# The sums and the gated product of a seven-product FFN move from GpSimd to VectorE, and its activation work is issued at fixed distances

## The chip, the cores and the metric

One core of one Trainium2 chip runs the whole program. The metric is device microseconds of one execution; the number quoted is a median over runs. All times are in microseconds (us) unless marked ns.

## The reference

A residual stream of 512 tokens by 1024 features goes through two blocks; all numbers are fp32. The first block is an HGRN2 mixer, a conv FFN, an NSA mixer and a conv FFN. The second is a SwiGLU FFN, a hybrid mixer and a SwiGLU FFN again. Only the two SwiGLU FFNs of the second block are touched by the change:

```python
def swiglu(x, w_gu, w_down):
    g, u = jnp.split(x @ w_gu, 2, axis=-1)
    return (jax.nn.silu(g) * u) @ w_down
```

Here x is 512 by 1024, w_gu is 1024 by 5632 and w_down is 2816 by 1024. The result, halved, is added to the stream.

## The kernel before

**How a product is made.** An fp32 product is made of three matmuls. Each operand is split into a high part in fp32r and the rest (h and l); the products h·h, h·l and l·h are added in PSUM. ScalarE writes the high part of a weight (line 249), VectorE the rest (line 250), so every weight piece costs one instruction on each. An activation is split in the same way (lines 473 and 476).

**The order.** The program writes its order by hand. Every engine runs its own instructions in the order in which the program issued them. Side work is a set of generators; a small queue (Weave) resumes them by a clock that advances with the matmuls issued, so `yield 1.2` means "go on 1.2 us of matmul work later". That clock only decides the order in which instructions stand on each engine.

**The seven products.** In the two SwiGLU FFNs the first two pairs of column tiles (t = 0 and 2) are ordinary: a block for the gate half g and a block for the up half u, evacuated by line 1146 (silu, ScalarE) and line 1168 (product, VectorE). From t = 4 on, that is for 9 of the 11 pairs of each FFN and 18 in all, a 2x2 block product is made with seven half-size products instead of eight (`fm_fast`, lines 463 to 465). This document calls such a pair of tiles a group, and each of the seven products a step. The steps of a group run in the order A11, A12, S2, S1, S3, S4, A22, each of 24 matmuls with 256 columns. They accumulate in the PSUM banks A, F, A, E, A, E, A. The bank A of one step has to be emptied before the step after next may start in it.

Per group the engines around TensorE do this:

- The weights arrive as four raw tiles of 128x1024 (5 buffers). `w_sum` makes four sums or differences of them, S1 to S4 (lines 210, 212, 215, 219; S1 and S2 in `wsum` tiles, S3 and S4 in place), on GpSimd.
- The seven weight pieces are split (lines 249 and 250) six pieces ahead of their use (HL_BUFS = 6).
- The banks are emptied after their steps: line 1109 (ScalarE, after A11), 1115 (ScalarE, after S2), 1112 (ScalarE, after S1), and 1117, 1120, 1122, 1127 (VectorE, after A12, S3, S4 and A22).
- silu runs on ScalarE right behind the VectorE add (lines 1118 and 1123), a product on GpSimd (line 1124), and the two results are split (473, 476) for the down product.

Ahead of the groups, `fast_inputs` makes sums of the normed input (lines 413 and 432 to 435) and splits them into the tiles T, with T_D as the distance between its parts. The stretch in which it runs, from the norm up to the first group, is called the ramp here. The groups come in rounds of 1, 4 and 4, each round followed by the down product, whose evacuation is line 790.

Of the kernel before, what the change touches and what calls it, by code (L numbers as in the profile page):

```python
# [12 lines left out]
F32 = mybir.dt.float32  # L13
F32R = mybir.dt.float32r
I32 = mybir.dt.int32
AF = mybir.ActivationFunctionType
OP = mybir.AluOpType
# [8 lines left out]
HALVES = ((0, 256), (256, 512))  # L26
FULL = ((0, 512),)
RAW_BUFS, SUM_BUFS, HL_BUFS, W2_BUFS = 5, 2, 6, 11
T_D, FAST_FROM = 1.2, 4
HG_D1, HG_D2, HG_D3, HG_D4, HG_D5 = 0.8, 1.9, 1.1, 0.0, 3.1  # L30
NORM_D1, NORM_D1B, NORM_D2, NORM_STEP, NHALF, W_DELAY, NPE = 1.6, 4.5, 1.2, 0.2, 2, 13.0, 7
W_UNIT = 29
# [86 lines left out]
class Builder:  # L119
# [81 lines left out]
    def w_sum(self, g, name):  # L201


        raw = lambda f: self.w_raw[g["load"] + ("A21", "A22", "A11", "A12").index(f)]
        src = g["src"]
        if name in ("S1", "S2"):
            src[name] = self.t([128, 4, 256], "wsum", SUM_BUFS)
        tt = self.nc.gpsimd.tensor_tensor
        if name == "S1":
            tt(src["S1"], raw("A21"), raw("A22"), op=OP.add)  # L210
        elif name == "S2":
            tt(src["S2"], src["S1"], raw("A11"), op=OP.subtract)
        elif name == "S3":
            src["S3"] = raw("A21")
            tt(src["S3"], raw("A11"), src["S3"], op=OP.subtract)
            self.raw_free()
        else:
            src["S4"] = raw("A12")
            tt(src["S4"], src["S4"], src["S2"], op=OP.subtract)
# [184 lines left out]
    def fast_inputs(self, X, tags, first, second):  # L404


        nc = self.nc
        xh, xl = X
        th, tl = self.big(tags[0], F32R), self.big(tags[1], F32R)
        two = lambda t: t.rearrange("p (i t) -> p i t", t=256)  # L410

        def whole(k, lo, f):
            nc.gpsimd.tensor_tensor(two(f), xh[:, k::4, lo:lo + 256].bitcast(F32), xl[:, k::4, lo:lo + 256].bitcast(F32),
                                    op=OP.add)
            return f

        def run():
            yield from self.wv.wait_in(first)
            yield 1.5
            left = []  # L420
            store = self.t([128, 1024], "hmask")
            for k in range(4):
                left.append(whole(k, 0, store[:, k * 512:k * 512 + 512] if k < 2 else self.w2()))
                yield T_D
            yield from self.wv.wait_in(second)
            yield 0.5
            for k in range(4):
                r, q = whole(k, 256, self.w2()), left[k]
                yield T_D
                a, b = self.w2(), self.w2()  # L430
                tt = nc.vector.tensor_tensor
                tt(a[:, 0:256], r[:, 0:256], q[:, 0:256], op=OP.subtract)
                nc.gpsimd.tensor_tensor(a[:, 256:512], r[:, 256:512], r[:, 0:256], op=OP.subtract)
                tt(b[:, 0:256], r[:, 256:512], a[:, 0:256], op=OP.subtract)
                tt(b[:, 256:512], q[:, 256:512], b[:, 0:256], op=OP.subtract)
                for i, f in enumerate((a, b)):
                    self.split(th[:, i * 4 + k, :], tl[:, i * 4 + k, :], f)
                    yield T_D
        return (th, tl), self.wv.spawn(run())

    def fm_fast(self, X, T, blocks, after):
# [643 lines left out]
    def ffn(self, X, waits, up, down, scale, after, conv=None, tags=None):  # L1085

        nc = self.nc
# [5 lines left out]
        pend = []  # L1093

        def fast_group(a, t):

            c = {}
            f = slice(t - a, t - a + 2)
            two = lambda w: w.rearrange("p (m t) -> p m t", t=256)

            def late(lo, src):
                yield 1.2
                self.split(mh[:, f, lo:lo + 256], ml[:, f, lo:lo + 256], two(src))

            def after(step, banks):
                A, E, F = (banks.get(n) for n in "AEF")
                if step == "A11":
                    c["1"] = self.w2()
                    nc.scalar.activation(c["1"], A, AF.Copy)
                elif step == "S1":  # L1110
                    c["5"] = self.w2()
                    nc.scalar.activation(c["5"], E, AF.Copy)
                elif step == "S2":
                    c["2"] = self.w2()
                    nc.scalar.activation(c["2"], A, AF.Copy)  # L1115
                elif step == "A12":
                    nc.vector.tensor_tensor(c["1"], c["1"], F, op=OP.add)
                    nc.scalar.activation(c["1"], c["1"], AF.Silu)
                elif step == "S3":
                    nc.vector.tensor_tensor(c["5"], c["5"], A, op=OP.add)  # L1120
                elif step == "S4":
                    nc.vector.tensor_tensor(c["2"], c["2"], E, op=OP.add)
                    nc.scalar.activation(c["2"], c["2"], AF.Silu)
                    nc.gpsimd.tensor_tensor(c["2"], c["2"], c["5"], op=OP.mult)
                    pend.append(self.wv.spawn(late(256, c["2"]), 1.2))
                else:
                    nc.vector.tensor_tensor(c["1"], c["1"], A, op=OP.mult)
                    pend.append(self.wv.spawn(late(0, c["1"])))
            self.fm_fast(X, T, ((up, 0, 8, t * 128, 256), (up, 0, 8, DFF + t * 128, 256)), after)

        for r, (a, b) in enumerate(self.ROUNDS):
            mh, ml = self.big("b0", F32R), self.big("b1", F32R)
# [997 lines left out]
```

## Time and profile before

| | |
|---|---|
| median of 3 runs | 2788.18 us (2786.33 to 2792.54) |
| the profiled execution: its own time | 2786.39 us |
| the profiled execution: span of its trace | 2784.6 us |
| TensorE busy | 2703.4 us, 97% of the span |
| VectorE, ScalarE, GpSimd busy | 61%, 41%, 19% |
| groups of the two SwiGLU FFNs | 1526 to 1808 and 2450 to 2730 us, with the down products between them |

The span is the time between the first and the last instruction in the trace; the execution took 1.8 us more. Busy shares are averages over stages that have different limits.

### The profile page before, as it was taken

To read this page: it belongs to the slowest core of one execution; us is meant where nothing else is said; L and a number is where in the kernel's file an instruction comes from. 1 tells how busy PE (TensorE), PEld (TensorE's weight loads), DVE (VectorE), ACT (ScalarE), POOL (GpSimd) and SP (SyncE) were. 2 spreads that over 40 slices of the span, in tenths; PEclk is the share of its full clock that TensorE was granted. 3 is DMA by queue.
4 is the path that set the end of the run, shared out by engine and by line. 5 is a ranking of instruction groups with operands and counts; after the bars stand their busy time and mean duration, and the time that the engine had idled before them with its cause. 6 is when DMAs were issued, how large, how long until landed. Compare 5 with 4: busy or idle time off the path is not lost.

```text
span 2784.6 us, 40263 instructions
## 1 busy us (share of the span) xinstructions
PE 2703.4 (97%) x15857; PEld 2358.7 (85%) x15857; DVE 1703.4 (61%) x2867; ACT 1142.0 (41%) x2114; POOL 533.8 (19%) x518
## 2 busy tenths in 40 slices
PE   7999999999999999999999989999999999998999
PEld 5988898888978889888888888897878987988888
DVE  7876567767545896544448675753455235768584
ACT  3323353323323895333344443442356333344343
POOL 3111110000102781000014333310000000425241
PEclk8999999999999999999999999999999999999999
DMA  7642136555231002333221332347535332222321
GB/s 260 191 143 84 46 99 198 178 185 175 64 106 61 1 2 76 100 105 99 91 91 50 110 103 81 106 68 118 95 86 82 60 91 91 69 91 91 106 92 61
DMA packets 257658, 278.94 MB, mean 100 GB/s; under 512 B 16408, under 2 KB 231853, under 8 KB 257469
## 3 DMA queue, kind: packets, MB, share of 16 engines
q1 hardware_dynamic: 229739, 233.23, 30.0%
q10 hardware_dynamic: 27730, 43.14, 5.0%
q8 instruction: 125, 2.05, 0.3%
q14 instruction: 64, 0.52, 0.1%
HBM read 274.23 MB, written 2.10 MB: 99 GB/s over the span
## 4 chain that ended last, share of the span: by engine, by line
PE 82%; DVE 11%; ACT 3%; issue 3%; POOL 1%; DMA 0%; ACTq 0%; DVEq 0%; SPq 0%; POOLq 0%
PE pg L363 20%; PE pg L364 20%; PE pg L366 20%; DVE wl L250 4%; PE pg L463 2%; PE pg L464 2%; PE pg L465 2%; PE pa L891 2%; DVE b L476 2%; ACT wh L249 1%; PE pg L395 1%; PE pg L393 1%; PE pg L394 1%; PE pa L1487 1%; DVE w L534 1%
## 5 line engine op out<-in xcount | busy, mean ns | idle before, releaser
L250 DVE TENSOR_TENSOR wl<-raw,wh 128x512 fp32r<-128x512 f32 (+2 forms) x806 | 649.2, 833 | 341.7 <-ACT wh L249 340.4
L363 PE MATMUL pg<-b,wh 128*128 128x512 f32 (+1 forms) x1856 | 673.5, 364 | 1.0 <-DVE w L1168 1.0
L364 PE MATMUL pg<-b,wl 128*128 128x512 f32 (+1 forms) x1856 | 668.0, 361 | 0.0
L249 ACT ACTIVATE wh<-raw 128x512 fp32r<-128x512 f32 (+2 forms) x806 | 495.7, 657 | 218.5 <-PE pg L366 142.0
L366 PE MATMUL pg<-b,wh 128*128 128x512 f32 (+1 forms) x1472 | 522.8, 357 | 0.0
L363 PE MATMUL pg<-hTh,wh 128*128 128x512 f32 (+2 forms) x1096 | 412.6, 378 | 9.3 <-DVE w L1168 7.3
L364 PE MATMUL pg<-hTh,wl 128*128 128x512 f32 (+2 forms) x1096 | 406.5, 373 | 0.7 <-DVE wl L250 0.5
L366 PE MATMUL pg<-hTl,wh 128*128 128x512 f32 (+2 forms) x1096 | 397.9, 370 | 0.0
L363 PEld LDWEIGHTS pg<-b,wh 128*128 128x128 f32 x1856 | 348.7, 188 | 56.7 <-DVE w L1168 1.4
L364 PEld LDWEIGHTS pg<-b,wl 128*128 128x128 f32 x1856 | 348.8, 188 | 54.7
L366 PEld LDWEIGHTS pg<-b,wh 128*128 128x128 f32 x1472 | 275.1, 188 | 44.1
L495 POOL TENSOR_TENSOR w<-w,w 128x256 f32<-128x256 f32 (+1 forms) x78 | 78.4, 1010 | 1153.5 <-ACT w L494 1152.9
L363 PEld LDWEIGHTS pg<-hTh,wh 128*128 128x128 f32 (+1 forms) x1096 | 206.3, 188 | 54.4 <-issue 12.7
L366 PEld LDWEIGHTS pg<-hTl,wh 128*128 128x128 f32 (+1 forms) x1096 | 203.3, 188 | 40.9 <-DVE hTl L476 0.4
L364 PEld LDWEIGHTS pg<-hTh,wl 128*128 128x128 f32 (+1 forms) x1096 | 206.4, 188 | 35.9 <-DVE wl L250 1.1
L473 ACT ACTIVATE b<-w 128x512 fp32r<-128x512 f32 (+1 forms) x128 | 77.2, 604 | 294.4 <-DVE w L1168 155.8
L463 PE MATMUL pg<-b,wh 128*128 128x256 f32 x576 | 167.5, 291 | 30.8 <-ACT w L1115 23.4
L465 PE MATMUL pg<-b,wl 128*128 128x256 f32 x576 | 165.6, 287 | 0.0
L464 PE MATMUL pg<-b,wh 128*128 128x256 f32 x576 | 165.4, 287 | 0.0
L476 DVE TENSOR_TENSOR b<-w,b 128x512 fp32r<-128x512 f32 (+1 forms) x128 | 124.2, 971 | 55.8 <-ACT b L473 55.3
L366 PE MATMUL pg<-hTh,wh 128*128 128x512 f32 (+1 forms) x384 | 142.7, 378 | 0.0
L463 PEld LDWEIGHTS pg<-b,wh 128*128 128x128 f32 x576 | 112.4, 195 | 34.8 <-ACT w L1115 25.1
(414 smaller groups left out, 4472.6 us busy)
## 6 DMA issues: line engine op xcount, KB each, us to landing
raw<-in_ffn_w_up_dram SPq DMA_DIRECT2D x88, 512.0 KB
raw<-in_ffn_w_gu_dram SPq DMA_DIRECT2D x88, 512.0 KB
w<-in_ada_w_dram ACTq DMA_DIRECT2D x160, 256.0 KB
raw<-in_ffn_w_down_dram SPq DMA_DIRECT2D x64, 512.0 KB
raw<-in_w_in_dram SPq DMA_DIRECT2D x64, 512.0 KB
raw<-in_hg_w_in_dram SPq DMA_DIRECT2D x32, 512.0 KB
raw<-in_ffn_w_down_dram SPq DMA_DIRECT2D x32, 384.0 KB
raw<-in_nsa_w_in_dram SPq DMA_DIRECT2D x20, 512.0 KB
```

Source lines behind the costliest of these rows:

```text
L249: nc.scalar.activation(h[:, k:e, :ncol], src[:, k:e, :ncol], AF.Copy)
L250: nc.vector.tensor_tensor(l[:, k:e, :ncol], src[:, k:e, :ncol], h[:, k:e, :ncol].bitcast(F32), op=OP.subtract)
L363: mm(p[:mw, :n], h[:, c], xh[:, k, lo:hi], start=k == 0, stop=False)
L364: mm(p[:mw, :n], l[:, c], xh[:, k, lo:hi], start=False, stop=False)
L366: mm(p[:mw, :n], at(j)[0][:, c], xl[:, j, lo:hi], start=False, stop=j == nk - 1)
L463: mm(o, h[:, k, c], xh, start=first and k == 0 and m == 0, stop=False, skip_group_check=True)
L464: mm(o, h[:, k, c], xl, start=False, stop=False, skip_group_check=True)
L465: mm(o, l[:, k, c], xh, start=False, stop=k == 3 and m == 1, skip_group_check=True)
L473: self.nc.scalar.activation(h, src, AF.Copy)
L476: self.nc.vector.tensor_tensor(l, src, h.bitcast(F32), op=OP.subtract)
L495: nc.gpsimd.tensor_tensor(acc[0][:, lo:hi], acc[0][:, lo:hi], sq[:, lo:hi], op=OP.add)
L891: mm(p[:, c, :n], s["k"][:, cc], q, start=True, stop=True)
```

## The change

Seven kinds of instructions go from GpSimd to VectorE: the four weight sums, the input sums of line 413, the difference of line 433, and the product of line 1124. T_D, the distance in `fast_inputs`, goes from 1.2 to 1.8. In `fast_group` the silu, the product and the two parts of the split, which were issued in one go, become generators with distances of their own.

```diff
-T_D, FAST_FROM = 1.2, 4
+T_D, FAST_FROM = 1.8, 4
...
 def w_sum(self, g, name):
-        tt = self.nc.gpsimd.tensor_tensor
+        tt = self.nc.vector.tensor_tensor
...
         def whole(k, lo, f):
-            nc.gpsimd.tensor_tensor(two(f), xh[:, k::4, lo:lo + 256].bitcast(F32), xl[:, k::4, lo:lo + 256].bitcast(F32),
+            nc.vector.tensor_tensor(two(f), xh[:, k::4, lo:lo + 256].bitcast(F32), xl[:, k::4, lo:lo + 256].bitcast(F32),
                                     op=OP.add)
...
-                nc.gpsimd.tensor_tensor(a[:, 256:512], r[:, 256:512], r[:, 0:256], op=OP.subtract)
+                tt(a[:, 256:512], r[:, 256:512], r[:, 0:256], op=OP.subtract)
...
-            def late(lo, src):
+            def silu(w):
+                yield 0.9
+                nc.scalar.activation(w, w, AF.Silu)
+
+            def out(lo, w, by=None):
+                if by is not None:
+                    yield 2.2
+                    nc.vector.tensor_tensor(w, w, by, op=OP.mult)
+                yield 0.9
+                h = mh[:, f, lo:lo + 256]
+                nc.scalar.activation(h, two(w), AF.Copy)
                 yield 1.2
-                self.split(mh[:, f, lo:lo + 256], ml[:, f, lo:lo + 256], two(src))
+                nc.vector.tensor_tensor(ml[:, f, lo:lo + 256], two(w), h.bitcast(F32), op=OP.subtract)
...
                 elif step == "A12":
                     nc.vector.tensor_tensor(c["1"], c["1"], F, op=OP.add)
-                    nc.scalar.activation(c["1"], c["1"], AF.Silu)
+                    self.wv.spawn(silu(c["1"]))
...
                     nc.vector.tensor_tensor(c["2"], c["2"], E, op=OP.add)
-                    nc.scalar.activation(c["2"], c["2"], AF.Silu)
-                    nc.gpsimd.tensor_tensor(c["2"], c["2"], c["5"], op=OP.mult)
-                    pend.append(self.wv.spawn(late(256, c["2"]), 1.2))
+                    self.wv.spawn(silu(c["2"]))
+                    pend.append(self.wv.spawn(out(256, c["2"], c["5"])))
                 else:
                     nc.vector.tensor_tensor(c["1"], c["1"], A, op=OP.mult)
-                    pend.append(self.wv.spawn(late(0, c["1"])))
+                    pend.append(self.wv.spawn(out(0, c["1"])))
```

The order of the instructions on TensorE and on SP's DMA queue is the same before and after. GpSimd only loses rows. The following pieces show VectorE and ScalarE; line numbers of the change are those of the new file, in which the bank adds 1117, 1120, 1122 are 1127, 1130, 1132 and the ScalarE copies 1109, 1112, 1115 are 1119, 1122, 1125.

VectorE around one group in the middle of a round (t = 8), before. The names are output<-inputs; `w_1985` is the tile that A11 and A12 fill, `w_1993` and `w_1997` those of S2/S4 and S1/S3, and `wl` is the rest of a weight piece.

```order
L250 TENSOR_TENSOR wl_14241<-raw_13883,wh_14240 128x1024
L1117 TENSOR_TENSOR w_1985_14233<-w_1985_14233,pg_13969 128x512
L250 TENSOR_TENSOR wl_14273<-raw_14175,wh_14272 128x1024
L250 TENSOR_TENSOR wl_14305<-raw_14208,wh_14304 128x1024
L250 TENSOR_TENSOR wl_14339<-wsum_14276,wh_14338 128x1024
L1120 TENSOR_TENSOR w_1997_14333<-w_1997_14333,pg_13967 128x512
L250 TENSOR_TENSOR wl_14368<-wsum_14238,wh_14367 128x1024
L1122 TENSOR_TENSOR w_1993_14299<-w_1993_14299,pg_13968 128x512
```

The same place in the change:

```order
L210 TENSOR_TENSOR wsum_14238<-raw_14017,raw_14082 128x1024
L250 TENSOR_TENSOR wl_14241<-raw_13883,wh_14240 128x1024
L1127 TENSOR_TENSOR w_1985_14233<-w_1985_14233,pg_13969 128x512
L250 TENSOR_TENSOR wl_14272<-raw_14173,wh_14271 128x1024
L212 TENSOR_TENSOR wsum_14275<-wsum_14238,raw_14173 128x1024
L250 TENSOR_TENSOR wl_14305<-raw_14206,wh_14304 128x1024
L215 TENSOR_TENSOR raw_14017<-raw_14173,raw_14017 128x1024
L219 TENSOR_TENSOR raw_14206<-raw_14206,wsum_14275 128x1024
L250 TENSOR_TENSOR wl_14339<-wsum_14275,wh_14338 128x1024
L1130 TENSOR_TENSOR w_1997_14333<-w_1997_14333,pg_13967 128x512
L250 TENSOR_TENSOR wl_14368<-wsum_14238,wh_14367 128x1024
L1132 TENSOR_TENSOR w_1993_14299<-w_1993_14299,pg_13968 128x512
```

The four sums now stand among the splits of the next group's pieces: S1's ahead of the split of this group's A22, S2's behind A11's, and S3's and S4's behind A12's.

ScalarE at the same group, before:

```order
L1109 ACTIVATE w_1985_14233<-pg_13967 128x512
L249 ACTIVATE wh_14240<-raw_13883 128x1024
L1118 ACTIVATE w_1985_14233<-w_1985_14233 128x512
L249 ACTIVATE wh_14272<-raw_14175 128x1024
L1115 ACTIVATE w_1993_14299<-pg_13967 128x512
```

In the change:

```order
L1119 ACTIVATE w_1985_14233<-pg_13967 128x512
L249 ACTIVATE wh_14240<-raw_13883 128x1024
L249 ACTIVATE wh_14271<-raw_14173 128x1024
L1103 ACTIVATE w_1985_14233<-w_1985_14233 128x512
L1125 ACTIVATE w_1993_14299<-pg_13967 128x512
```

The silu of the first half (1118, now 1103) moves behind one weight split. It still stands ahead of the copy that empties bank A after S2 (1115, now 1125).

VectorE at the end of the ramp of the first of the two FFNs, before, up to the line 1168 that empties the first bank of the up block of t = 0 (its second half of tokens):

```order
L434 TENSOR_TENSOR w_1860_13282<-w_1856_13259,w_1859_13281 128x256
L435 TENSOR_TENSOR w_1860_13282<-hmask_13024,w_1860_13282 128x256
L476 TENSOR_TENSOR b_1822_13001<-w_1859_13281,b_1821_13000 128x512
L250 TENSOR_TENSOR wl_13295<-raw_12762,wh_13294 128x512
L476 TENSOR_TENSOR b_1822_13001<-w_1860_13282,b_1821_13000 128x512
L250 TENSOR_TENSOR wl_13295<-raw_12762,wh_13294 128x512
L250 TENSOR_TENSOR wl_13339<-raw_12980,wh_13338 128x512
L432 TENSOR_TENSOR w_1869_13345<-w_1864_13323,w_1829_13053 128x256
L434 TENSOR_TENSOR w_1870_13346<-w_1864_13323,w_1869_13345 128x256
L435 TENSOR_TENSOR w_1870_13346<-w_1829_13053,w_1870_13346 128x256
L476 TENSOR_TENSOR b_1822_13001<-w_1869_13345,b_1821_13000 128x512
L1168 TENSOR_TENSOR w_1836_13085<-w_1836_13085,pg_13267 128x256
```

In the change, up to the same instruction (1177 in the new file):

```order
L413 TENSOR_TENSOR w_1859_13284<-hTh_12504,hTl_12505 128x512
L250 TENSOR_TENSOR wl_13287<-raw_12762,wh_13286 128x512 x2
L432 TENSOR_TENSOR w_1862_13310<-w_1859_13284,hmask_13024 128x256
L433 TENSOR_TENSOR w_1862_13310<-w_1859_13284 128x256
L434 TENSOR_TENSOR w_1863_13311<-w_1859_13284,w_1862_13310 128x256
L435 TENSOR_TENSOR w_1863_13311<-hmask_13024,w_1863_13311 128x256
L476 TENSOR_TENSOR b_1822_13001<-w_1862_13310,b_1821_13000 128x512
L210 TENSOR_TENSOR wsum_13332<-raw_13032,raw_13236 128x1024
L250 TENSOR_TENSOR wl_13335<-raw_12980,wh_13334 128x512
L1177 TENSOR_TENSOR w_1835_13083<-w_1835_13083,pg_13265 128x256
```

`fast_inputs` works on its second half in four parts. Before, three of them stood ahead of that bank's product (the fence begins inside the second); now two do, together with one weight sum.

## Rows read from the trace of the kernel before

**Rows 1.** The page, part 1: busy time, share of the span, instructions.

```profile
PE 2703.4 (97%) x15857; PEld 2358.7 (85%) x15857; DVE 1703.4 (61%) x2867; ACT 1142.0 (41%) x2114; POOL 533.8 (19%) x518
```

**Rows 2.** TensorE's waits, 1582 to 2735 us: total, times, longest.

```profile
PE pg L463 <- ACT w L1115: 23.4, 8, 2.9
PE pg L463 <- ACT w L1109: 4.4, 7, 1.0
...
PE pg L463 <- DVE w L1120: 1.1, 2, 0.6
```

**Rows 3.** Timeline of TensorE: start, duration, instruction, idle time before it and releaser.

```profile
1609.26 0.39 PE L463 MATMUL pg<-b,wh 128*128 128x256 f32 x1 [0.56 <-ACT w L1109]
...
1614.78 0.28 PE L464 MATMUL pg<-b,wh 128*128 128x256 f32 x1
1614.90 0.28 PE L465 MATMUL pg<-b,wl 128*128 128x256 f32 x1
1618.11 0.39 PE L463 MATMUL pg<-b,wh 128*128 128x256 f32 x1 [2.93 <-ACT w L1115]
...
1645.12 0.41 PE L463 MATMUL pg<-b,wh 128*128 128x256 f32 x1
1645.33 0.41 PE L464 MATMUL pg<-b,wh 128*128 128x256 f32 x1
```

**Rows 4.** Windows: PE, PEld, DVE, ACT, POOL busy (instructions), granted clock, DMA, GB/s.

```profile
1643.00:1653.00 10.00, 10.00 (x73) 10.00 (x73) 7.92 (x7) 4.76 (x6) 3.65 (x2) 0.83 0.16 54
```

**Rows 5.** Timeline of ScalarE in the same group.

```profile
1616.00 0.63 ACT L1118 ACTIVATE w<-w 128x512 f32<-128x512 f32 x1 [5.84 <-DVE w L1117]
...
1617.48 0.58 ACT L1115 ACTIVATE w<-pg 128x512 f32<-128x512 f32 x1
```

**Rows 6.** Timeline of VectorE in the same group.

```profile
1603.17 1.47 DVE L250 TENSOR_TENSOR wl<-raw,wh 128x1024 fp32r<-128x1024 f32 x1 [1.65 <-ACT wh L249]
...
1607.38 0.67 DVE L1127 TENSOR_TENSOR w<-w,pg 128x512 f32<-128x512 f32 x1
1607.98 1.21 DVE L250 TENSOR_TENSOR wl<-raw,wh 128x1024 fp32r<-128x1024 f32 x1
1609.12 2.90 DVE L476 TENSOR_TENSOR b<-w,b 128x512 fp32r<-128x512 f32 x1
1611.94 3.42 DVE L250 TENSOR_TENSOR wl<-raw,wh 128x1024 fp32r<-128x1024 f32 x1
1615.29 0.67 DVE L1117 TENSOR_TENSOR w<-w,pg 128x512 f32<-128x512 f32 x1
```

**Rows 7.** Timeline of GpSimd in the same group.

```profile
1608.30 3.17 POOL L212 TENSOR_TENSOR wsum<-wsum,raw 128x1024 f32<-128x1024 f32 x1 [1.39 <-DMA raw<-in_ffn_w_gu_dram]
1611.42 2.86 POOL L215 TENSOR_TENSOR raw<-raw,raw 128x1024 f32<-128x1024 f32 x1
```

**Rows 8.** Window of one whole group, columns as in rows 4.

```profile
1609.26:1633.95 24.69, 20.76 (x169) 20.14 (x169) 20.99 (x14) 10.73 (x15) 13.00 (x6) 1.00 0.27 86
```

**Rows 9.** GpSimd's groups by line and shape: busy, mean ns, idle before.

```profile
L210 POOL TENSOR_TENSOR wsum<-raw,raw 128x1024 f32<-128x1024 f32 x18 | 55.1, 3060 | 66.6 <-DMA raw<-in_ffn_w_gu_dram 42.9 <-DVE wl L250 23.7
...
L219 POOL TENSOR_TENSOR raw<-raw,wsum 128x1024 f32<-128x1024 f32 x18 | 44.4, 2465 | 103.2 <-DVE wl L250 95.0 <-issue 8.3
...
L1124 POOL TENSOR_TENSOR w<-w,w 128x512 f32<-128x512 f32 x18 | 23.3, 1296 | 169.3 <-ACT w L1123 169.3
```

**Rows 10.** Timeline of VectorE in the first FFN's ramp.

```profile
1499.04 2.63 DVE L432 TENSOR_TENSOR w<-w,hmask 128x256 f32<-128x256 f32 x1
```

**Rows 11.** Timeline of TensorE in the two ramps.

```profile
1513.76 0.47 PE L363 MATMUL pg<-hTh,wh 128*128 128x512 f32 x1 [3.95 <-DVE w L1168]
...
1534.33 0.38 PE L463 MATMUL pg<-b,wh 128*128 128x256 f32 x1 [1.96 <-ACT w L1109]
...
2438.14 0.47 PE L363 MATMUL pg<-hTh,wh 128*128 128x512 f32 x1 [3.39 <-DVE w L1168]
...
2457.31 0.38 PE L463 MATMUL pg<-b,wh 128*128 128x256 f32 x1 [0.55 <-ACT w L1109]
```

## The prediction

> **What bounds the kernel now.** The page's first part comes first: TensorE is busy for 2703.4 of 2784.6 us [rows 1]. A change that issues the same matmuls can therefore win only where TensorE stands still or runs slowly, so the next view is its waits, in the stretch that holds the groups. There the reader sees one line, 463 (the first matmul of a step), and three releasers: ScalarE's copy 1115 (23.4 us, 8 times), its copy 1109 (4.4 us, 7 times) and VectorE's add 1120 (1.1 us, twice) [rows 2]. All three empty a bank.
>
> Such a wait is followed back through one group. TensorE stops for 2.93 us at 1618 for the copy 1115 [rows 3]. ScalarE did that copy at 1617.48, right behind the silu 1118, which had waited 5.84 us for VectorE's add 1117 [rows 5]. VectorE did the add only at 1615.29, although TensorE had finished A12 by 1608.70, where it began to wait for the copy 1109 (1609.26 - 0.56) [rows 3]. Just ahead of it stand a subtraction of 512 columns that took 2.90 us and one of 1024 columns that took 3.42 us [rows 6]. The same two forms take 0.67 and 1.21 us elsewhere in these rows. What differs is GpSimd: its sums ran from 1608.30 to 1611.47 and from 1611.42 to 1614.28 [rows 7], and the two long instructions end just when these do. So VectorE stands still while GpSimd works through its own sum. That is why a group of which VectorE's own work is 11.6 us (below) keeps VectorE busy for 20.99 us [rows 8].
>
> **Cost of the group's part.** VectorE's instructions begin 0.60 us apart at 512 columns (1607.38 to 1607.98) and 1.14 us apart at 1024 (1607.98 to 1609.12) [rows 6]. A group has seven splits of 1024 columns, four adds and two splits of 512: 7 x 1.14 + 6 x 0.60 = 11.6 us. The change adds four sums of 1024 columns and a product of 512. The trace has none of them on VectorE. The nearest rows are the splits, which also read two SBUF tiles: 4 x 1.14 + 0.60 = 5.2 us. The other bound is GpSimd's price, 2.47 to 3.06 us a sum and 1.30 us the product [rows 9]: 11.2 to 13.5 us, 12.4 in the middle. I take 5.2, since it is the engine and not the operation that sets the time in rows 6. VectorE then needs 16.8 us per group. TensorE's 168 matmuls, 0.12 us apart (1614.78 to 1614.90) [rows 3], need 20.2 us.
>
> Does the order hold inside a group? A step is 24 matmuls, 2.9 us. I walk VectorE through one, from the end of A11. S1's sum takes it to 1.5, and the split of A22 (whose high part ScalarE writes first, about 1.06 us) to 2.8. The add 1117 can start at 2.95, that is 0.1 us after A12 instead of 6.6 us now (1608.70 to 1615.29). Behind it come a split and S2's sum, to 6.2; after S2 a split and two sums, to 10.8; after S1 a split, to 11.9; after S3 the add and a split, to 13.7; after S4 the add, a split and the product, to 17.2; after A22 the product, a split and two splits of activations, to 20.7, which is 0.5 us into the next group. The copy 1115 gives the bank back one step after S2. The add 1117 could slip by about 4 us before the silu behind it made that copy late. So all the waits of rows 2 go.
>
> The sums wait for weights now on VectorE, with the splits queued behind them and the bank adds behind those. In this group A11's raw tile landed at 1608.30 [rows 7], 3.7 us after the split that frees a buffer was done (1603.17 + 1.47) [rows 6]. In the walk that split is done 2.2 us after S4, the tile lands at 5.9 and its first reader comes three steps after S4, at 8.6: 2.7 us to spare. At the start of a round the sum S1 waits for its two tiles; there VectorE is still busy with the splits of the round before when they land. I cost these waits at nothing; if the cover failed, VectorE would lose the part of 3.7 us that sticks out.
>
> Now the sum. The waits of rows 2 are 28.9 us, 0.55 of which belongs to the second ramp [rows 11]: 28.3 us in 16 waits. The gap between two matmuls at such a wait is 3.21 us where it would be 0.12 (1614.90 to 1618.11), 0.16 more than the wait [rows 3]: 16 x 0.16 = 2.6 us. After six of the eight long waits the granted clock falls to the lower of its two levels, 1.2 GHz, for about 3.4 us. One of the six such windows of 10 us shows 0.83 [rows 4], and matmuls stand 0.21 us apart there (1645.12 to 1645.33). Some 15 matmuls lose 0.095 us each, 1.4 us a time, 8.4 us in all. Together: 28.3 + 2.6 + 8.4 = **39.3 us**.
>
> **Cost of the ramp's part.** TensorE waits 3.95 and 1.96 us in the first ramp, 3.39 and 0.55 us in the second [rows 11]. VectorE's backlog is behind each: line 432 takes 2.63 us for 256 columns [rows 10], where 512 take 0.67 in rows 6. Ten instructions of the first ramp lose 13.4 us in this manner (the longest is that one) and eleven of the second 13.8 us. What VectorE takes on per ramp is eight sums of line 413 (0.60), four of line 433 (0.45, an estimate for half the columns of a 0.60) and four weight sums (1.14): 11.2 us. So VectorE comes out of the ramp 2.2 to 2.6 us earlier, and up to 4.9 us if its own idle time in the ramp (about 2 us, waits for ScalarE) shrinks too. I take 3.5 us each. The first wait of each ramp goes, since one part fewer stands ahead of that product and the backlog has 9 us to clear. But TensorE then arrives sooner at the step S2 of the first group and waits there some 3 us for the copy 1109. That copy is behind VectorE's last products of t = 2. So the ramp's gain is what VectorE gains, 7 us. From it goes 1.4 us for one clock drop in the second ramp, which has only the one behind its first wait today: **5.5 us**.
>
> T_D only spreads the input sums: their last splits stand in VectorE's row ahead of the products of t = 2 as before, so no wait is forced. GpSimd loses 114 instructions (72 + 16 + 8 + 18) and gets none, so nothing new waits for it. At the end of a round the last splits are forced out without their distances; the down product reads these tiles only after some 36 of its matmuls, over 7 us, which hides them.
>
> Sum: 2786.4 - 39.3 - 5.5 = 2741.6 us for an execution like the profiled one. The median of the runs was 1.8 us above it, which gives **2743 us**.
>
> **The rivals.** *VectorE too full.* It would be at 16.8 of 20.2 us, in order. If waits for ScalarE add 4 us in some groups, the copy 1115 is late again. Half of the group's gain gone makes 2763 us. For it: VectorE waits for ScalarE's high parts in almost every step already. Against it: in the walk the slack at 1117 is larger than any one instruction that remains.
>
> *The time is only moved.* If a sum on VectorE cost as much as the standstill that it ends, 9.4 us per group (20.99 - 11.6), nothing would change: 2788 us. The Trainium skill, Perfetto Trace Analysis, Optimizing Scalar/DVE Operations, warns that moving work between GpSimd and VectorE might not help because they share an SBUF read port. By that rule the time stays; rows 6 to 8 agree that the engines exclude each other, but put 5.2 us against 9.4.
>
> *Slower.* VectorE becomes the bound of the groups if the five added operations cost it GpSimd's price: 11.6 + 12.4 = 24.0 us against the 22.4 us that a group takes TensorE today (20.2 + 39.3/18), 1.6 us in each of 18 groups, or 2817 us. It decides from 10.8 us for the five. Against it: no VectorE instruction of 1024 columns in rows 6 takes over 1.5 us when GpSimd rests.
>
> *More is freed.* All of the ramp's waits go too, with their clock drops, and matmuls come 0.005 us closer together while GpSimd rests (they stand 0.115 us or less apart in a few steps of the first groups): 10 us and up to 15 us more, so 2718 to 2733 us.
>
> **How the numbers follow.** The forecast has 0.70, too full 0.16, more freed 0.07, only moved 0.03, slower 0.04. The range reaches from 2729 us, inside the freer case, to 2764 us, the too-full one at half of its gain; what lies outside is the last two cases and some of the freer one. A change of 0.2% (5.6 us) is about what a measurement can tell. Faster: 0.70 + 0.16 + 0.07 = 0.93; same 0.03; slower 0.04.
>
> **What would show it.** Right: no wait of line 463 for 1115 or 1120's successors in the middle of rounds; splits of 1024 columns at 1.2 us throughout the groups; sums on VectorE at 1.2 us; VectorE near 17 us busy per group; GpSimd some 255 us less busy (the page's 534 to about 280); a wait of about 3 us left at the first S2 of each FFN; a clock of 1.00 in the rounds. Wrong: the adds behind 1117 still several us after their step, with VectorE waiting for a DMA or busy without a gap; sums of over 2 us; or a first group that waits longer than today.

## The result, and the profile after

The changed kernel took **2739.2 us** in the median of 4 runs (2737.1 to 2741.91), the kernel before 2787.26 us on the same chip (2785.97 to 2792.54): a ratio of 0.9825, with a 95% interval of 0.9808 to 0.9842. The prediction was 2743 us, with a range of 2729 to 2764 us.

The page's first part answers to [rows 1]:

```profile
span 2737.5 us, 40163 instructions
...
PE 2688.7 (98%) x15857; PEld 2349.8 (86%) x15857; DVE 1671.8 (61%) x2981; ACT 1144.0 (42%) x2114; POOL 279.9 (10%) x404
```

VectorE has 114 instructions more and is busy for 31.6 us less. GpSimd is down by 253.9 us. TensorE's waits from 1470 to 2735 us, which cover the ramps and the groups and answer to [rows 2] and [rows 11] (total, times, longest):

```profile
PE pg L463 <- ACT w L1119: 5.4, 2, 3.4
...
PE pg L363 <- ACT w L1155: 0.7, 1, 0.7
```

Both rows belong to the ramps. Inside the four rounds of four groups nothing waits any more. The windows below run from a round's first matmul to its last, columns as in [rows 4]. Two of the four rounds of the kernel before:

```profile
1582.84:1672.66 89.82, 82.40 (x673) 81.31 (x671) 69.82 (x54) 41.87 (x57) 35.57 (x15) 0.98 0.33 106
1716.72:1806.65 89.93, 83.53 (x672) 82.79 (x671) 69.69 (x54) 41.88 (x57) 35.62 (x15) 0.96 0.33 106
```

The same two rounds of the change:

```profile
1580.23:1659.63 79.40, 79.40 (x672) 79.40 (x671) 63.26 (x69) 42.34 (x57) 0.00 (x0) 1.00 0.39 120
1703.70:1783.10 79.40, 79.40 (x673) 79.40 (x671) 63.26 (x69) 42.33 (x57) 0.00 (x0) 1.00 0.39 120
```

TensorE is now busy for the whole of a round. The four took 89.82, 89.93, 90.06 and 89.94 us, together 359.75, and take 4 x 79.40 = 317.60: **42.15 us** less. VectorE does 69 instructions in less time than 54 took. In the middle of a round, where [rows 6] showed standstills, VectorE's timeline now reads:

```profile
1604.87 1.22 DVE L250 TENSOR_TENSOR wl<-raw,wh 128x1024 fp32r<-128x1024 f32 x1
1606.06 0.69 DVE L1127 TENSOR_TENSOR w<-w,pg 128x512 f32<-128x512 f32 x1
1607.08 1.23 DVE L250 TENSOR_TENSOR wl<-raw,wh 128x1024 fp32r<-128x1024 f32 x1 [0.33 <-ACT wh L249]
1608.22 1.22 DVE L212 TENSOR_TENSOR wsum<-wsum,raw 128x1024 f32<-128x1024 f32 x1
```

A12's last matmul ran from 1605.74 to 1606.02, and its bank's add (1127, the old 1117) starts 0.04 us later. It was 6.6 us late in [rows 3, 6]. On ScalarE the copy that empties bank A after S2 (1125, the old 1115 of [rows 5]) now waits for TensorE:

```profile
1608.88 0.60 ACT L1125 ACTIVATE w<-pg 128x512 f32<-128x512 f32 x1 [1.32 <-PE pg L465]
```

The rest of the gain is in the ramps. I measure one from the first of the norm's small matmuls ahead of the FFN (line 518) to the first matmul of its first round of four, so the first, single group is in it. Both were 121.24 and 113.12 us, and are 117.98 and 111.21 us: **5.2 us** less. Rounds and ramps make 47.3 us; the two spans differ by 47.1.

### The profile page after: what moved, and what is told of

It reads as the page before. It is cut to its first block, busy times and chain, and to the rows that moved or that the text cites. A ratio compares the mean times of both kernels' runs of the same rounds, so it can differ in the third digit from the quotient of the medians.

```text
span 2737.5 us, 40163 instructions
## 1 busy us (share of the span) xinstructions
PE 2688.7 (98%) x15857; PEld 2349.8 (86%) x15857; DVE 1671.8 (61%) x2981; ACT 1144.0 (42%) x2114; POOL 279.9 (10%) x404
## 4 chain that ended last, share of the span: by engine, by line
PE 90%; DVE 5%; ACT 2%; issue 1%; SPq 1%; DMA 1%; POOL 0%; ACTq 0%; DVEq 0%; POOLq 0%
PE pg L363 21%; PE pg L364 21%; PE pg L366 20%; PE pg L464 4%; PE pg L465 4%; PE pg L463 4%; PE pa L891 2%; PE pg L395 1%; PE pg L394 1%; PE pg L393 1%; PE pa L1496 1%; DVE wl L250 1%; PE pa L1539 1%; PE pg L1454 1%; PE pg L1455 1%
## 5 line engine op out<-in xcount | busy, mean ns | idle before, releaser
L250 DVE TENSOR_TENSOR wl<-raw,wh 128x512 fp32r<-128x512 f32 (+2 forms) x806 | 592.9, 762 | 324.5 <-ACT wh L249 323.0
L363 PEld LDWEIGHTS pg<-b,wh 128*128 128x128 f32 x1856 | 348.5, 188 | 57.0 <-DVE w L1177 1.4
L366 PEld LDWEIGHTS pg<-b,wh 128*128 128x128 f32 x1472 | 275.2, 188 | 43.7
L463 PE MATMUL pg<-b,wh 128*128 128x256 f32 x576 | 162.9, 283 | 5.4 <-ACT w L1119 5.4
L464 PE MATMUL pg<-b,wh 128*128 128x256 f32 x576 | 162.5, 282 | 0.0
L473 ACT ACTIVATE b<-w 128x512 fp32r<-128x512 f32 (+1 forms) x92 | 54.4, 594 | 240.4 <-DVE w L1177 151.1
L464 PE MATMUL pg<-hTl,wh 128*128 128x256 f32 x432 | 122.6, 284 | 0.0
L463 PE MATMUL pg<-hTh,wh 128*128 128x256 f32 x432 | 121.3, 281 | 0.0
```

The source lines that it names most:

```text
L250: nc.vector.tensor_tensor(l[:, k:e, :ncol], src[:, k:e, :ncol], h[:, k:e, :ncol].bitcast(F32), op=OP.subtract)
L363: mm(p[:mw, :n], h[:, c], xh[:, k, lo:hi], start=k == 0, stop=False)
L366: mm(p[:mw, :n], at(j)[0][:, c], xl[:, j, lo:hi], start=False, stop=j == nk - 1)
L463: mm(o, h[:, k, c], xh, start=first and k == 0 and m == 0, stop=False, skip_group_check=True)
L464: mm(o, h[:, k, c], xl, start=False, stop=False, skip_group_check=True)
L473: self.nc.scalar.activation(h, src, AF.Copy)
```

## The experiments

Four ways to explain the gain were told apart. *A*: VectorE stands still while GpSimd reads SBUF, and sums on VectorE end that. *B*: the fixed distances, which move silu, product and split, do it. *C*: what counts is the lateness of the product or of the input sums. *D*: nothing stands still; a split merely waits for a slow sum of GpSimd. After the third run a fifth came up, *E*: the place of the sums in GpSimd's queue decides, not their engine.

Three of the twelve kernels do extra work, which their parts below name; the others do the change's work in another way. Ratios are to the kernel before on the same chip. "Rounds" is the sum of the four rounds, "ramps" that of the two ramps, from each kernel's profile.

| kernel | median us | ratio, 95% interval | rounds | ramps |
|---|---|---|---|---|
| before | 2787 to 2790 | 1 | 359.75 | 234.4 |
| the change | 2739.2 | 0.9825 (0.9808 to 0.9842) | 317.60 | 229.2 |
| engines alone | 2738.19 | 0.9818 (0.9803 to 0.9832) | 317.6 | 225.1 |
| distances alone | 2766.42 | 0.9918 (0.9903 to 0.9933) | 338.0 | 237.0 |
| weight sums back | 2746.71 | 0.9848 (0.9833 to 0.9863) | 317.6 | 238.3 |
| product back | 2740.62 | 0.9828 (0.9812 to 0.9845) | 317.6 | 229.2 |
| product alone | 2747.7 | 0.9849 (0.9832 to 0.9865) | 319.3 | 233.5 |
| weight sums alone | 2740.43 | 0.9820 (0.9802 to 0.9837) | 317.6 | 226.7 |
| product behind the sum | 2749.01 | 0.9859 (0.9843 to 0.9876) | 320.6 | 234.9 |
| first group ordinary | 2735.56 | 0.9817 (0.9802 to 0.9831) | 317.5 | 224.3 |
| the same, engines alone | 2737.38 | 0.9806 (0.9789 to 0.9823) | 317.5 | 224.3 |

The ramps repeat well: the change and "product back", whose ramps are the same but for one product, agree to 0.1 us in them. What lies ahead of the ramps, which no kernel here touches, differs by some us from one execution to the next (the first ramp began at 1460 to 1470 us), so medians closer than about 4 us are not told apart.

**The two halves.** Engines alone: the change without T_D = 1.8 and without the generators; the product is moved where it stood.

```diff
 T_D, FAST_FROM = 1.2, 4
...
-                    nc.gpsimd.tensor_tensor(c["2"], c["2"], c["5"], op=OP.mult)
+                    nc.vector.tensor_tensor(c["2"], c["2"], c["5"], op=OP.mult)
```

> The kernel before with the sums and the product on VectorE, but with silu, product and split issued as before and T_D at 1.2. Theory A (VectorE stands still while GpSimd reads SBUF, and the bank copies are late for that reason alone): nearly the whole gain, 2738 to 2746 us; the waits of line 463 in the middle of rounds go. Rival B (the waits came from silu and split standing in the way on ScalarE and VectorE): most of the gain is missing, 2765 to 2788 us, and waits for the copy behind the silu remain.

Distances alone: the change with every moved instruction back on GpSimd.

```diff
-        tt = self.nc.vector.tensor_tensor
+        tt = self.nc.gpsimd.tensor_tensor
...
-                    nc.vector.tensor_tensor(w, w, by, op=OP.mult)
+                    nc.gpsimd.tensor_tensor(w, w, by, op=OP.mult)
```

> The change's distances and T_D = 1.8 with every moved operation back on GpSimd. Theory A: no gain to speak of, 2775 to 2795 us, since VectorE's long splits of 2.9 to 3.4 us remain. Rival B: 2740 to 2765 us.

The engines alone give the whole gain. But the distances alone give half of the rounds' too (359.75 to 338.0), with all sums still on GpSimd. Theory A as I held it had not allowed for that. In this kernel TensorE waits for the copy 1125 for 1.5 us a time (12.0 us, 8 times) where it was 2.9 us in [rows 2]. The product still waits 4.16 us for its silu; the add after A12 still comes late, 5.3 us behind A12's last matmul instead of 6.6. Of the 21.8 us that the rounds gain, 12.7 are shorter waits. Most of the rest is the clock, which stays at 1.00 in all four rounds; the first one and that add:

```profile
1583.20:1667.77 84.57, 80.62 (x672) 79.76 (x671) 69.05 (x54) 42.46 (x57) 35.35 (x15) 1.00 0.37 113
...
1614.39 0.67 DVE L1127 TENSOR_TENSOR w<-w,pg 128x512 f32<-128x512 f32 x1
```

Which of the distances takes the 1.3 us off the add was not tried further.

**One kind of instruction back.** From the change, the four weight sums go back to GpSimd; or, in another kernel, only the product.

```diff
         src = g["src"]
-        tt = self.nc.vector.tensor_tensor
+        tt = self.nc.gpsimd.tensor_tensor
```

> The change with the four weight sums alone back on GpSimd (72 instructions of 2.5 to 3.1 us in the kernel before). Theory A: they make the larger part of the standstill, so 30 to 45 us of the gain go: 2770 to 2785 us, with waits in the middle of rounds again. Rival C (only the product's late result and the input sums mattered): 2739 to 2745 us.

```diff
-                    nc.vector.tensor_tensor(w, w, by, op=OP.mult)
+                    nc.gpsimd.tensor_tensor(w, w, by, op=OP.mult)
```

> The change with the product alone back on GpSimd (18 instructions of 1.3 us). Theory A: VectorE stands still for at most 1.3 us per group, less than the 4 us of slack that the walk gives at the add after A12, so no change: 2737 to 2743 us. Rival C (the product's late result was what mattered): 2755 us or more.

The first diff is that of the weight sums, the second that of the product. Each leaves the rounds at 79.4 us. For the weight sums that was a miss, and the telling one: VectorE still stands still. Its groups by form (busy, mean ns, idle before) in one round of the kernel before:

```profile
L250 DVE TENSOR_TENSOR wl<-raw,wh 128x1024 fp32r<-128x1024 f32 x18 | 29.1, 1627 | 12.2 <-ACT wh L249 12.2
L250 DVE TENSOR_TENSOR wl<-wsum,wh 128x1024 fp32r<-128x1024 f32 x6 | 13.7, 2284 | 0.8 <-ACT wh L249 0.8
L476 DVE TENSOR_TENSOR b<-w,b 128x512 fp32r<-128x512 f32 x6 | 12.9, 2156 | 0.0
```

The same round with the weight sums back:

```profile
L250 DVE TENSOR_TENSOR wl<-raw,wh 128x1024 fp32r<-128x1024 f32 x18 | 30.8, 1714 | 6.1 <-ACT wh L249 6.1
L250 DVE TENSOR_TENSOR wl<-wsum,wh 128x1024 fp32r<-128x1024 f32 x6 | 13.9, 2322 | 1.5 <-ACT wh L249 1.5
...
L1113 DVE TENSOR_TENSOR b<-w,b 128x512 fp32r<-128x512 f32 x6 | 3.8, 680 | 0.0
```

The weight splits are as slow as before. Only the splits of activations (476, now 1113) are back at 0.68 us, and that was enough. The reason is in GpSimd's queue. Its timeline, and VectorE's beside it, in the kernel before, just ahead of [rows 6, 7]:

```profile
1602.27 1.29 POOL L1124 TENSOR_TENSOR w<-w,w 128x512 f32<-128x512 f32 x1 [4.16 <-ACT w L1123]
1603.52 3.39 POOL L210 TENSOR_TENSOR wsum<-raw,raw 128x1024 f32<-128x1024 f32 x1
...
1604.57 2.89 DVE L476 TENSOR_TENSOR b<-w,b 128x512 fp32r<-128x512 f32 x1
1607.38 0.67 DVE L1127 TENSOR_TENSOR w<-w,pg 128x512 f32<-128x512 f32 x1
```

GpSimd waits 4.16 us for the silu 1123, because the product stands at the head of its queue. S1's sum stands behind it (without the product it starts some 4 us earlier, below) and so runs just when VectorE has the split 476 to do, which takes 2.89 us instead of 0.68. That delay lets the next sum, S2's, begin at 1608.30 while VectorE still has the second split 476 and a weight split ahead of the add 1117: the two slow instructions of [rows 6]. That is theory E.

**One kind alone.** It says that moving the product alone must do, although it is the cheapest of the five kinds that a group has (1.30 us against 2.47 to 3.06 us a sum), and moving the weight sums alone as well. Both from the kernel before, with old distances:

```diff
-                    nc.gpsimd.tensor_tensor(c["2"], c["2"], c["5"], op=OP.mult)
+                    nc.vector.tensor_tensor(c["2"], c["2"], c["5"], op=OP.mult)
```

> The kernel before, with the product of line 1124 alone on VectorE; all sums stay on GpSimd and silu, product and split keep their old places. Amount of GpSimd's work: six sums of 2.4 to 3.4 us (18 x 4 of them) still stop VectorE where they fall, the copy 1115 is late as before: rounds 88 to 90 us, 2778 to 2789 us in all. Place in GpSimd's queue: S1's sum no longer stands behind a product that waits 4.16 us for silu, so it runs some 4 us earlier, the sums end before the add 1117 is due, and the rounds fall to 79.4 to 83 us: 2745 to 2762 us.

```diff
         src = g["src"]
-        tt = self.nc.gpsimd.tensor_tensor
+        tt = self.nc.vector.tensor_tensor
```

> The kernel before, with the four weight sums alone on VectorE; product and input sums stay on GpSimd, all distances are the old ones. If the weight sums on GpSimd are what stops VectorE in the groups, and the product's 1.3 us does nothing: rounds 79.4 us, the ramps as before or up to 5 us better: 2739 to 2746 us. If sums and product must both go: rounds 82 us and more, over 2750 us.

Both do. The second also leaves product and input sums on GpSimd with rounds of 79.4 us, as "product back" did with the product, so C falls for the rounds. With the product alone, the same place of the program reads, GpSimd first:

```profile
1599.64 2.40 POOL L210 TENSOR_TENSOR wsum<-raw,raw 128x1024 f32<-128x1024 f32 x1 [1.21 <-DVE wl L250]
1610.31 3.15 POOL L212 TENSOR_TENSOR wsum<-wsum,raw 128x1024 f32<-128x1024 f32 x1 [8.27 <-DMA raw<-in_ffn_w_gu_dram]
...
1605.37 1.23 DVE L250 TENSOR_TENSOR wl<-raw,wh 128x1024 fp32r<-128x1024 f32 x1 [0.26 <-ACT wh L249]
1606.52 0.69 DVE L476 TENSOR_TENSOR b<-w,b 128x512 fp32r<-128x512 f32 x1
...
1608.85 0.69 DVE L476 TENSOR_TENSOR b<-w,b 128x512 fp32r<-128x512 f32 x1
...
1611.07 0.68 DVE L1117 TENSOR_TENSOR w<-w,pg 128x512 f32<-128x512 f32 x1
1613.40 4.65 DVE L250 TENSOR_TENSOR wl<-raw,wh 128x1024 fp32r<-128x1024 f32 x2 [1.65 <-ACT wh L249]
```

S1's sum no longer waits for the silu. In both kernels S2's sum begins 3.7 us after the weight split that frees a buffer for its tile (1604.64 to 1608.30 before, 1606.60 to 1610.31 here). In the kernel before, S1's sum takes 2.2 us of these 3.7 from VectorE; here VectorE has both splits 476 behind it when S2's sum comes. The add 1117, with one input in PSUM, keeps its 0.68 us and is 2.3 us late instead of 6.6. What is stretched now is two weight splits that nobody needs soon.

**The place.** This test moves nothing off GpSimd. In the kernel before, the product is issued later, so that in the third and fourth group of a round it stands behind S1's sum. Its split moves along with it.

```diff
+                if by is not None:
+                    yield 6.0
+                    nc.gpsimd.tensor_tensor(src, src, by, op=OP.mult)
+                    yield 2.0
...
-                    nc.gpsimd.tensor_tensor(c["2"], c["2"], c["5"], op=OP.mult)
-                    pend.append(self.wv.spawn(late(256, c["2"]), 1.2))
+                    pend.append(self.wv.spawn(late(256, c["2"], c["5"])))
```

> The kernel before with everything left on GpSimd; only the product of line 1124 is issued 5 us of matmul work later or more, so that in the third and fourth group of a round it stands behind the next group's sum S1 in GpSimd's queue, and its split follows 2 us later. If the place of the product in GpSimd's queue is what makes the sums late: S1's sum starts right behind the sum before it, the copy 1115 is early again and the rounds fall to 80 to 84 us: 2742 to 2765 us. If it is GpSimd's work as such that stops VectorE, whatever its order: rounds 88 to 90 us, 2778 to 2789 us.

The rounds fall to 80.1 to 80.2 us, 39.2 of the change's 42.15 us, with GpSimd busy for 34.2 us of a round (35.6 before). GpSimd's timeline shows the new order; what stands behind the waiting product now is a sum that waits for its weights anyway. Two rows of VectorE's stand below it:

```profile
1603.59 2.40 POOL L210 TENSOR_TENSOR wsum<-raw,raw 128x1024 f32<-128x1024 f32 x1 [1.22 <-DVE wl L250]
1608.42 1.29 POOL L1104 TENSOR_TENSOR w<-w,w 128x512 f32<-128x512 f32 x1 [2.43 <-ACT w L1128]
1614.53 2.52 POOL L212 TENSOR_TENSOR wsum<-wsum,raw 128x1024 f32<-128x1024 f32 x1 [4.82 <-DMA raw<-in_ffn_w_gu_dram]
...
1614.67 0.68 DVE L1122 TENSOR_TENSOR w<-w,pg 128x512 f32<-128x512 f32 x1
...
1620.43 0.68 DVE L476 TENSOR_TENSOR b<-w,b 128x512 fp32r<-128x512 f32 x1
```

So the place in GpSimd's queue is not all that differs: the product's split 476 now stands behind the add after A12 (1122 in this file), which takes 0.6 us of undisturbed work out of that add's way. The kernel with the product alone on VectorE left this split ahead of the add, so it is the cleaner test of E.

**Does GpSimd really stop VectorE, and by what?** To the change, work is added on GpSimd behind four of the seven splits of a group, for which nobody waits. Once it reads SBUF, four adds of 128x256:

```diff
...
+            for j in range(4):
+                nc.gpsimd.tensor_tensor(s, s, l[:, j, :].bitcast(F32), op=OP.add)
```

> The change with work added on GpSimd that nobody waits for: behind four of the seven weight splits of a group, four additions of 128x256 that read the split's result in SBUF and write a scratch tile. Theory A (VectorE's instructions with two SBUF inputs stand still while GpSimd reads SBUF): the splits grow from 1.2 us to 2 us and more, VectorE needs up to 12 us more per group and the waits return: 2765 to 2850 us. Rival D (before, the slow sums themselves were waited for, and GpSimd's mere activity costs nothing): 2737 to 2743 us.

Once it only fills it, nine times 128x256, but for one column that it reads:

```diff
...
+            nc.gpsimd.tensor_tensor(s[:, 0:1], s[:, 0:1], l[:, 0, 0:1].bitcast(F32), op=OP.add)
+            for _ in range(9):
+                nc.gpsimd.memset(s, 0.0)
```

> The same places and about the same time on GpSimd, but with nine fills of 128x256 that read nothing (behind one addition of a single column, which ties them to the split). Theory A in the narrow form (what excludes is GpSimd's reading): no change, 2737 to 2743 us. Theory A in a wide form (any GpSimd access to SBUF excludes): as with the additions, 2765 us or more.

Reads: 2779.2 us (ratio to before 0.9974, 0.9965 to 0.9983), rounds of 86.6 to 88.2 us, 40 us lost. Fills: 2739.03 us (0.9832, 0.9815 to 0.9848), rounds of 79.40 us, nothing lost. The load is not equal: GpSimd is busy for 77 of the 87.4 us of the first round with the reads and for 45 of 79.4 us with the fills. What tells them apart is that the 1024-column splits of a round with fills take 1.22 us in the mean, as without them. VectorE's timeline with the reads:

```profile
1612.97 0.68 DVE L1134 TENSOR_TENSOR w<-w,pg 128x512 f32<-128x512 f32 x1
1613.57 1.21 DVE L250 TENSOR_TENSOR wl<-raw,wh 128x1024 fp32r<-128x1024 f32 x1
1614.70 1.77 DVE L212 TENSOR_TENSOR wsum<-wsum,raw 128x1024 f32<-128x1024 f32 x1
1616.39 1.76 DVE L250 TENSOR_TENSOR wl<-raw,wh 128x1024 fp32r<-128x1024 f32 x1
1618.08 1.76 DVE L215 TENSOR_TENSOR raw<-raw,raw 128x1024 f32<-128x1024 f32 x1
```

An instruction that lasts 1.22 us elsewhere takes 1.76, while the bank add, which has one input in SBUF and one in PSUM, keeps its 0.68. No wait of VectorE or ScalarE in the first round with reads ends at a GpSimd instruction, so neither is held by a split's result that GpSimd still reads. The Trainium skill, SBUF — State Buffer, Who interferes with whom, states that a VectorE instruction with two SBUF inputs contends with a GpSimd instruction that reads SBUF, and not with one that only writes it. The stretch from 1.22 to 1.76 us beside the reads, and the fills that cost nothing, agree with it. So A's mechanism holds, and D falls: in the kernel before, nothing that the two slow instructions of [rows 6] read came from GpSimd.

**How much room has VectorE?** To the change, four repeats of S2's sum per group are added on VectorE, all at one place (more work than the reference asks for).

```diff
+            for _ in range(4):
+                tt(src["S2"], src["S1"], raw("A11"), op=OP.subtract)
             src["S3"] = raw("A21")
```

> The change with four more sums per group on VectorE (S2 computed five times): VectorE needs 16.8 + 4 x 1.14 = 21.4 us per group where TensorE needs 19.9. If VectorE's work is what fills a group (the rival of a VectorE that is too full), the 16 groups of the full rounds take 1.5 us more each: 2755 to 2775 us. If VectorE has more room than the walk says, 2737 to 2745 us.

A miss: 2817.62 us (1.0112, 1.0097 to 1.0127), rounds of 94.4 to 97.0 us. A full group of the change keeps VectorE busy as follows (columns as in [rows 4]):

```profile
1600.08:1619.93 19.85, 19.85 (x170) 19.85 (x170) 17.25 (x19) 10.96 (x14) 0.00 (x0) 1.00 0.35 106
```

2.6 us per group are free. Four more sums, begun 1.14 us apart, are 4.56: 2.0 us too much. The rounds grew by 4.2 us per group. TensorE now waits twelve times for the add after S3 (the row below; this file's 1132 is the change's 1130), and the granted clock over the first round is 0.91. Of the 66 us that the four rounds grew, gaps of over 0.24 us between matmuls make 44, and matmuls 0.16 to 0.24 us apart make 22. My expectation had left the second part out.

```profile
PE pg L465 <- DVE w L1132: 40.0, 12, 3.6
...
1585.38:1682.37 96.99, 87.08 (x673) 86.45 (x671) 77.32 (x81) 42.31 (x57) 0.00 (x0) 0.91 0.31 98
```

**The ramp.** The change keeps two waits at the first group. Here that group (t = 4) is an ordinary pair; once from the change, once from the engines alone (T_D 1.2).

```diff
-T_D, FAST_FROM = 1.8, 4
+T_D, FAST_FROM = 1.8, 6
```

> The change with the pair t = 4 of each FFN made as an ordinary product, so that the seven-product groups begin in the second round, long after the input sums. The two waits of 3.44 and 1.97 us for the copy after A11 and the two clock drops behind them (1.5 to 2 us each) should go, 8 to 9 us, less some 1 us because an ordinary pair takes 20.5 us and a group 19.9: 2730 to 2734 us. If the waits only move to another place of the ramp: 2737 to 2743 us.

> The engine moves alone (old distances, T_D 1.2), with the pair t = 4 of each FFN made as an ordinary pair too. As the same step won 3.6 us on the full change by taking its waits of 3.4 and 2.0 us at the first S2 away: here there was one such wait of 3.5 us, so 2734 to 2737 us. If the pair's own extra matmuls (8 half products in place of 7, some 2.9 us a pair) eat the gain: 2738 to 2742 us.

The waits are gone. The ramps are 4.9 us shorter than the change's, less than I expected, and only 0.8 us shorter than with the engines alone. What I had missed is the price of the pair: I had taken 20.5 us for it, but its 96 matmuls of 512 columns stand 0.232 us apart and need 22.3 us, where the group needs 19.85. A window inside the pair of the first kernel:

```profile
1522.00:1544.00 22.00, 22.00 (x96) 17.76 (x95) 7.90 (x14) 6.29 (x14) 0.00 (x0) 1.00 0.29 91
```

These are the fastest medians of the study, 2735.56 and 2737.38 us; their intervals overlap with the change's.

## Why the prediction was right

**The bound and the path** held. TensorE won where it waited, the three releasers of [rows 2] are gone from the rounds, and matmuls in a round stand as close as before (0.118 us in the mean), so the rival in which more is freed did not come.

**The standstill** as a mechanism is shown by the reads and the fills. The step from it to the gain was incomplete, though. I wrote that VectorE stands still while GpSimd works through its sum and let the gain follow from ending that. In three kernels (weight sums back, product alone, product behind the sum) the weight splits still stand still, and the rounds are as short or nearly so. What must go is only the standstill between the start of A11 and the add 1117, and it came from a queue: S1's sum behind a product that waits 4.16 us for a silu, and then S2's sum, which finds VectorE not yet done. [Rows 9] had the sign of it, 169.3 us of idle time ahead of line 1124, and I read only its price. The two long instructions of [rows 6] do not end just when GpSimd's sums do, as I wrote, but at 1612.02 and 1615.36, the sums at 1611.47 and 1614.28 [rows 7]. The difference, 0.55 and 1.08 us, is about what each takes undisturbed.

**VectorE's terms.** I took 5.2 us for the five added instructions, and 16.8 us per group. The sums last 1.22 us and begin 1.13 to 1.14 us apart, the product 0.69; a full group keeps VectorE busy for 17.25 us. The choice between the two bounds, by the engine and not by the operation, was right; GpSimd's price would have been 12.4 us. One argument for it was weak: GpSimd rested through neither of the 1024-column splits of [rows 6] that took under 1.5 us (they began at 1603.17 and 1607.98, sums at 1603.52 and 1608.30). The walk's add came 0.04 us after A12 (forecast 0.1), and no sum waited for a weight: of the four groups of sums on VectorE, all with no idle time ahead, one reads:

```profile
L212 DVE TENSOR_TENSOR wsum<-wsum,raw 128x1024 f32<-128x1024 f32 x18 | 22.0, 1220 | 0.0
```

**The rounds' sum** was 39.3 us and came out as 42.15. The waits with their excess gaps were 30.9 us by my sum, and adding up every gap of over 0.24 us between matmuls in the four rounds of before gives 30.9. The clock, forecast at 8.4 us, came close too: in the six drops 97 matmuls stand 0.21 us apart and lose 8.9 us to the usual 0.12, 1.5 us a drop. What I had left out is 2.1 us in 21 more such gaps at full clock, most of them the second gap behind a wait, as from the first to the second of these matmuls:

```profile
1642.80 0.39 PE L463 MATMUL pg<-b,wh 128*128 128x256 f32 x1 [2.93 <-ACT w L1115]
1643.02 0.28 PE L464 MATMUL pg<-b,wh 128*128 128x256 f32 x1
```

**The ramp's sum** was 5.5 us and came out as 5.2: the first waits of 3.95 and 3.39 us [rows 11] are gone but for 0.7, and waits of 3.4 and 2.0 us are left at the first S2, each with a clock drop behind it. Here are the second and its window:

```profile
2429.96 0.39 PE L463 MATMUL pg<-b,wh 128*128 128x256 f32 x1 [1.97 <-ACT w L1119]
...
2430.00:2440.00 10.00, 10.00 (x72) 10.00 (x73) 5.45 (x8) 5.16 (x10) 0.00 (x0) 0.83 0.65 198
```

But this near hit is partly luck. The engine moves alone shorten the two ramps by 9.3 us (234.4 to 225.1), more than I took. I costed T_D and the distances at nothing, and they take 4.1 us of it back: with the engines alone the second ramp has no such wait (107.87 us against 111.21). Which of the two does it, T_D or the generators, was not tried apart. In the working, 2.6 us and idle time of about 2 us make 4.6 us, not 4.9; the 3.5 us that I took lies inside either.

**The rivals.** VectorE is not too full, but 2.6 us per group is all that is left. "Only moved" is refuted: VectorE does more and is busy for less. That the distances (B) carry the gain is refuted by the engines alone; that they could carry half of it without any move is the part I had not seen. E does not explain that half either: in that kernel the product stands ahead of S1's sum and waits 4.16 us as before.

## What to carry to other kernels

Where an engine stands still because another reads SBUF, ask first which of these standstills lies ahead of something that TensorE waits for, and then why the other engine works just then: here one cheap instruction at the head of a queue, waiting for a silu, held back the sums behind it. Moving that one instruction, or issuing it and its split later, gave nearly as much as moving seven kinds. And count what fills an engine after the move: 17.25 of 19.85 us is a group that holds, and 2 us beyond its end cost 4.2 us a group here, in part because the matmuls behind TensorE's waits ran at the lower clock.

## What was not expected of the hardware

- GpSimd's fills next to VectorE cost it nothing (splits of 1.22 us, rounds of 79.40 us, with 126 fills per round), while GpSimd's reads of SBUF stretch VectorE's instructions with two SBUF inputs from 1.22 to 1.76 us and up to 3.4 us [rows 6], and leave those with one input in PSUM at 0.68 us.
- A wait of TensorE of 2 to 3.4 us was followed by a granted clock of 0.70 to 0.83 over the next 10 us in both ramps of the change; in the rounds of before, six of eight waits of 2.9 us were followed by the lower of the two levels, 1.2 GHz, at 1.5 us a drop on top of the wait, and eight waits of 1.5 us (distances alone) by none, with a clock of 1.00.
- In an ordinary pair matmuls of 512 columns stand 0.232 us apart, in a group two of 256 columns 0.236 us: a group without waits takes 19.85 us where the pair takes 22.3.
